# A hybrid SSD/attention layer with a convolutional FFN: TensorE's order ahead of the FFN written by hand

## The chip, the cores and the metric

One core of a Trainium2 chip runs the whole program in one launch. The metric is the device time of an execution in microseconds; of the kernel before there are three timed runs and one profiled execution.

## What is computed

One inference step of a one-layer streaming encoder for two groups of requests that share weights: a prompt of 2048 frames, and a sample group of 8 streams with 16 frames each and 512 cached positions. All data is float32.

```python
n = rmsnorm(x, norm1_g)
z, xbc, dt_raw, q, k, v, f_raw = split_columns(n @ w_in)     # 1024 -> 512,1024,8,512,512,512,8
y_ssd = ssd_mixer(z, xbc, dt_raw, ...)    # conv of width 4, SiLU, Mamba-2 scan (8 heads, state 128), gated norm
logf  = log_sigmoid(f_raw + fox_f_bias)
y_fox = softmax(q k' / 8 + F_q - F_k, causal) v              # F = cumsum(logf); 8 heads of 64
h = x + concat(y_ssd, y_fox) @ w_out
u = causal_dwconv(rmsnorm(h, norm2_g) @ w_up)                # 1024 -> 2 x 2816, width 3
y = rmsnorm(h + (silu(u_g) * u_v) @ w_down, final_norm_g)
# also returned: new k, v, logf, SSD state and both conv states of either group
```

## The kernel before

The 2048 prompt frames and the 128 sample frames (16 x 8) are 17 tiles of 128 rows; tile SMP holds the sample frames. Ahead of the FFN the prompt is worked in four parts of 512 rows (two windows of 256; the sample tile rides with part 0). Each matrix product with weights is done as three matmuls, high by high, high by low and low by high of operands split in two (`split`, one copy and one subtraction).

For each part p:
- `a_head(p)`: norm of the rows, written as high and low into the tiles nT0 and nT1 (one buffer each). A sum of squares per tile (ScalarE), a power on POOL, a scaled identity `dg`, a matmul that spreads it over partitions (line 196), a multiply with the transposed rows xT (line 202), the split.
- `a_body(p)`, first half: `proj_tm` (v and the gate columns, token-major, lines 344 to 346), `gates` (softplus, log-sigmoid and cumulative sums by a chain of small VectorE operations and small matmuls, lines 244 to 323), and `proj_cm` for four pairs of q and k (column-major, through `mm3`, lines 114 to 116). q and k go to DRAM as high and low.
- `attention(p)`: for each of 8 heads `s_phase` computes scores with queries on partitions (line 589) to get each row's maximum (line 592), which is transposed (603), copied out (605), stored to DRAM in st_d (606) and fetched back into row 66 and 67 of the q tile (607), so that `t_phase` gets transposed scores with the maximum already subtracted (629, 630), takes the exponential on ScalarE (636) and weighs v two units late (618). A unit is one block of 128 keys by 512 queries; a head of part p has 4(p+1). The PSUM tag s has four buffers, pv one, mm three. `ssd_chunk` steps (scan of one tile; for SMP a loop over 8 states in the tag yl) are issued between the units.
- for part 0, `sample_attention` behind the part's attention: per sequence, scores against 512 cached and 16 new keys, exponential, four transposes (757), weighing (768).
- `a_body(p)`, second half: `proj_cm` for 8 tiles of x with the convolution, `proj_tm` for z.

Then w_out is loaded and `out_proj` runs over the tiles, and the FFN follows in three groups of tiles (w_up, convolution, SiLU, w_down).

The order of every engine's queue, TensorE's too, is chosen when the kernel is built: a planner takes the traced instructions, with the order of tracing as priority, and simulates their times. Loads of data, stores and fetches all go through SP's DMA queue; weights go through ScalarE's.

Of the kernel before, what the change touches and what calls it, by code (L numbers as in the profile page):

```python
# [17 lines left out]
P = 128  # L18
# [9 lines left out]
H = 8  # L28
# [22 lines left out]
XB = 1  # L51
QB = 4
PB = 4
# [13 lines left out]
def hybrid_step(ctx: ExitStack, tc: tile.TileContext, i: dict, o: dict):  # L67
# [17 lines left out]
    st_d = dram.tile([H, 4, 2, 512], F32, name="st_d")  # L85
# [67 lines left out]
    def a_head(p, prev):  # L153
        res = []
        first = p == 0
        for e, w in enumerate(part_windows(p)):
            W = win_width(w, PAD1)
            wt = at([P, 2, KT, W], f"nT{e}", 1, F32R)
            if prev is None:
                V.memset(wt[:, :, :, 0:PAD1].bitcast(F32), 0.0)  # L160
            else:
                pw, pt = prev
                ed = PAD1 + pw[1] - pw[0]
                V.tensor_copy(wt[:, :, :, 0:PAD1], pt[:, :, :, ed - PAD1:ed].bitcast(F32))
            groups = [(w[0] // P, 2, PAD1, i["xTw"][w[0] // 256])]
            if w[2]:
                sb = PAD1 + w[1] - w[0]
                groups.append((SMP, 1, sb, i["xTs"]))
            for c0, n, col, xsrc in groups:
                N = n * P  # L170
                pr = tpt()
                if first:
                    xa = at([P, 2, KT, P], "cmw", WA).rearrange("p c k d -> p c (k d)")
                    for c in range(n):
                        nc.scalar.dma_start(xa[:, c], i["xr"][c0 + c])
                xTs = []
                for kk in range(0, KT, 4):
                    xT = at([P, 4, 256], "qk" if first else "xT", 2 if first else 1)
                    if first:
                        dma(xT[:, :, :N], xsrc[:, kk:kk + 4])  # L180
                    xTs.append(xT)
                for c in range(n):
                    ss = at([P, 2], "ss", 2)
                    if first:
                        S.activation(xa[:, c], xa[:, c], AF.Square, accum_out=ss[:, 0:1])
                    else:
                        for hf in range(2):
                            xt = at([P, 512], "xt", XB)
                            dA(xt, i["xr"][c0 + c][:, hf * 512:(hf + 1) * 512])
                            S.activation(xt, xt, AF.Square, accum_out=ss[:, hf:hf + 1])  # L190
                        V.tensor_add(ss[:, 0:1], ss[:, 0:1], ss[:, 1:2])
                    ss = ss[:, 0:1]
                    rsq(ss, D)
                    dg = at([P, P], "dg", 1)
                    V.tensor_scalar_mul(dg, ident, ss)
                    T.matmul(pr[:, c * P:(c + 1) * P], ones, dg, start=True, stop=True)
                for kk in range(0, KT, 4):
                    xT = xTs[kk // 4]
                    if not first:
                        dma(xT[:, :, :N], xsrc[:, kk:kk + 4])  # L200
                    for k in range(4):
                        V.scalar_tensor_tensor(xT[:, k, :N], xT[:, k, :N], g1c[:, kk + k:kk + k + 1], pr[:, :N],
                                               op0=ALU.mult, op1=ALU.mult)
                    split(xT[:, :, :N], wt[:, 0, kk:kk + 4, col:col + N], wt[:, 1, kk:kk + 4, col:col + N], S,
                          V if first and kk else G)
            prev = (w, wt)
            res.append(prev)
        wins_of[p] = res
        return prev

    def gates(p, dtf):
# [29 lines left out]
        if p == 0:  # L241
            dS(o["logf"][:, SMP], lf[:, 4])
        pc = tpt()
# [16 lines left out]

        an = at([P, 40], "g_an", 1)
# [14 lines left out]
        split(nf.rearrange("p c h -> p (c h)"), nh[:, 0], nh[:, 1], V, V)  # L276
        for a in range(2):
# [5 lines left out]
            dS(k2_d[:, 64 + a, p * 512:(p + 1) * 512], fr)  # L283
        if p > 0:
            return
# [6 lines left out]
        clf = at([P, 512], "xT", 1)  # L292
# [13 lines left out]
        split(snf.rearrange("p b h c -> p (b h c)"), snh[:, 0], snh[:, 1], V, V)  # L306
        pr = tpt()
        for a in range(4):
            T.transpose(pr[:, a * P:(a + 1) * P], snh[:, a // 2, (a % 2) * P:(a % 2 + 1) * P].bitcast(F32), ident)
        snr = at([P, 512], "xT", 1)  # L310
# [9 lines left out]
        split(ow, owh[:, 0], owh[:, 1], V, V)  # L320
        pr = tpt()
# [4 lines left out]
    def a_body(p):  # L326

        wins = wins_of[p]

        def proj_tm(src, n, use):  # L330
# [7 lines left out]
            for w, wt in wins:  # L338
                for c in win_tiles(w):
                    ps = mmt()  # L340
                    a = PAD1 + (c * P if c != SMP else w[1]) - w[0]
                    for k in range(KT):
# [3 lines left out]
                        T.matmul(ps[:, :n], wt[:, 1, k, a:a + P], we[:, 0, :n], start=False, stop=k == KT - 1)  # L346
                    use(ps, c)

# [31 lines left out]
        def proj_cm(ct, use, pad):  # L380
            wc = load_cm(ct)
            for w, wt in wins:
                W = win_width(w, PAD1) - PAD1 + pad
                ps = mmt()
                mm3(ps, lambda k: wc[:, 0, k, :], lambda k: wc[:, 1, k, :], wt[:, :, :, PAD1 - pad:], W, KT)
                use(ps, w, W)

# [56 lines left out]
        for pair in range(4):  # L444
            proj_cm(pair, use_qk(0, pair), 0)
            proj_cm(4 + pair, use_qk(1, pair), 0)
        yield
        for ct in range(8):
            proj_cm(8 + ct, use_x(ct), PAD1)
        proj_tm(i["w_tm"][1], 256, use_z(0))  # L450
        proj_tm(i["w_tm"][2], 256, use_z(1))
        if p == NPART - 1:
            dS(o["conv1"], cs1)
        yield


    def ssd_chunk(c):
# [51 lines left out]
        else:  # L509
            for b in range(NB):  # L510
                yield
# [5 lines left out]
                              xb[:, 6:8].rearrange("p g (t b) -> p g t b", b=NB)[:, :, :, b])  # L517
                for g in range(2):
                    T.matmul(po[:, g * 256:(g + 1) * 256], cm[:, g], s0[:, g * 256:(g + 1) * 256],
                             start=b == 0 and g == 0, stop=b == NB - 1 and g == 1, skip_group_check=True)  # L520
                xeb = bt_([P, 512], "pr", PB)
                V.tensor_scalar_mul(xeb, xe, blkb[:, b:b + 1])
# [56 lines left out]
    def s_phase(h, qb, done):  # L579

        q12 = load_q(h, qb)
        nm = bt_([P, 4, 4], "nm", 2)
        for kb in range(qb + 1):
            ks = load_ks(h, kb)
            for qi in range(4):
                W = (qi + 1) * P if kb == qb else 512
# [25 lines left out]
    def t_phase(h, qb, q12, yl, dn):  # L612
        pv = psb.tile([P, 512], F32, tag="pv", name="pv", bufs=1)
        order = [qb] + list(range(qb))
        late = []

        def weigh(vr, jj, of, pr, first, last):
# [571 lines left out]
```

## Time and profile before

| | us |
|---|---|
| median of 3 runs | 3202.15 (3199.07 to 3204.54) |
| the profiled execution, whole | 3197.92 |
| its span, first to last instruction | 3196.2 |
| TensorE busy | 3030.4 (95%) |
| VectorE busy | 1787.8 (56%) |
| ScalarE busy | 1029.7 (32%) |
| POOL busy | 899.0 (28%) |

Matmuls are pipelined and their ends modelled, so busy matmul time is not matmul time at peak. "Idle" is time with no matmul in flight. The granted clock of a stretch is a mean over two levels, 1.00 (2.4 GHz) and 0.50 (1.2 GHz). The span holds two halves: the stages ahead of the FFN up to about 1600 us, and the FFN.

### The profile page before, as it was taken

The page shows a single profiled execution, that of the slowest core. Times are in us where ns is not written, and L with a number is a line of the kernel's source. Part 1 is how long each engine was busy: PE and PEld are TensorE (multiplying, and loading weights), DVE is VectorE, ACT ScalarE, POOL GpSimd, SP SyncE. Part 2 cuts the span into 40 slices and gives each one's busy share as a digit, 9 for nine tenths or more (in the row PEclk, how much of TensorE's full clock was granted, in tenths as well). Part 3 has the DMA queues.
Part 4 walks back from the last instruction along what each step waited for, and adds up shares of the span by engine and source line. Part 5 has one row for each costly group of instructions (what it writes and reads, how often), then busy time and mean ns, then how long its engine had stood idle before and what let it go on. Part 6 is the DMA issues. An engine that isn't in the chain of part 4 may idle for free.

```text
span 3196.2 us, 45570 instructions
## 1 busy us (share of the span) xinstructions
PE 3030.4 (95%) x17712; PEld 2671.9 (84%) x17712; DVE 1787.8 (56%) x3315; ACT 1029.7 (32%) x1778; POOL 899.0 (28%) x580
## 2 busy tenths in 40 slices
PE   3999799798999998999999999999999999999999
PEld 3987688577777875777799999999999999999998
DVE  5175346654664465452455555566555556766666
ACT  2344333433444344322232222234222223422322
POOL 3222232322232323110132322223232222333332
PEclk8999899899999999999999999999999999999999
DMA  3757675646454746542621221223121221322221
GB/s 134 221 178 231 207 214 172 183 145 197 149 162 139 216 143 187 163 156 96 234 90 55 75 60 62 67 84 115 53 66 60 73 60 67 112 80 79 68 70 68
DMA packets 234495, 398.63 MB, mean 125 GB/s; under 512 B 62944, under 2 KB 119144, under 8 KB 234280
## 3 DMA queue, kind: packets, MB, share of 16 engines
q1 hardware_dynamic: 180712, 234.48, 23.3%
q10 hardware_dynamic: 53568, 161.24, 16.1%
q8 instruction: 140, 2.29, 0.3%
q14 instruction: 75, 0.61, 0.1%
HBM read 317.26 MB, written 78.38 MB: 124 GB/s over the span
## 4 chain that ended last, share of the span: by engine, by line
PE 83%; DMA 10%; DVE 4%; issue 1%; SPq 1%; ACT 1%; POOL 0%; ACTq 0%; DVEq 0%; POOLq 0%
PE mm L115 14%; PE mm L114 14%; PE mm L116 14%; PE pv L618 6%; PE dn L904 5%; PE dn L905 5%; PE dn L906 5%; PE s L629 2%; PE s L630 2%; PE dn L804 2%; PE dn L805 2%; PE dn L806 2%; PE mm L346 2%; PE s L589 2%; PE mm L344 2%; PE mm L345 2%
## 5 line engine op out<-in xcount | busy, mean ns | idle before, releaser
L106 POOL TENSOR_TENSOR wr<-raw,wr 128x1024 fp32r<-128x1024 f32 x198 | 476.4, 2414 | 1032.5 <-ACT wr L103 1025.0
L114 PE MATMUL mm<-nT,wr 128*128 128x386 f32 (+1 forms) x2112 | 696.4, 330 | 1.3 <-ACT wr L103 0.8
L115 PE MATMUL mm<-nT,wr 128*128 128x386 f32 (+1 forms) x2112 | 695.3, 329 | 0.1
L116 PE MATMUL mm<-nT,wr 128*128 128x386 f32 (+1 forms) x2112 | 694.4, 329 | 0.0
L882 DVE SCALAR_TENSOR_TENSOR ac<-mm,cw,ac 128x384 f32<-128x384 f32 (+1 forms) x528 | 301.6, 572 | 345.0 <-ACT ac L880 337.3
L880 ACT ACTIVATE ac<-mm,cw 128x384 f32<-128x384 f32 (+1 forms) x264 | 172.8, 654 | 786.1 <-PE mm L116 783.5
L115 PEld LDWEIGHTS mm<-nT,wr 128*128 128x128 f32 x2112 | 399.3, 189 | 6.8 <-DVE nT L106 0.3
L907 DVE TENSOR_TENSOR y<-y,dn 128x512 f32<-128x512 f32 x374 | 255.1, 684 | 267.3 <-PE dn L906 264.6
L114 PEld LDWEIGHTS mm<-nT,wr 128*128 128x128 f32 x2112 | 397.5, 188 | 7.7 <-ACT wr L103 1.1
L116 PEld LDWEIGHTS mm<-nT,wr 128*128 128x128 f32 x2112 | 397.9, 188 | 5.7
L106 POOL TENSOR_TENSOR cmw<-craw,cmw 128x1024 fp32r<-128x1024 f32 (+1 forms) x96 | 232.3, 2422 | 378.0 <-ACT cmw L103 304.8
L114 PE MATMUL mm<-nT,cmw 128*128 128x256 f32 (+2 forms) x1024 | 307.7, 300 | 1.8 <-ACT ev L400 1.8
L116 PE MATMUL mm<-nT,cmw 128*128 128x256 f32 (+2 forms) x1024 | 305.4, 298 | 0.0
L115 PE MATMUL mm<-nT,cmw 128*128 128x256 f32 (+2 forms) x1024 | 305.4, 298 | 0.0
L904 PE MATMUL dn<-wr,ht 128*128 128x512 f32 x748 | 294.4, 394 | 2.9 <-DVE y L907 1.7
L618 PE MATMUL pv<-pr,v 128*128 128x512 f32 (+3 forms) x640 | 291.9, 548 | 2.6 <-issue 1.4
L905 PE MATMUL dn<-wr,ht 128*128 128x512 f32 x748 | 292.8, 391 | 0.0
L906 PE MATMUL dn<-wr,ht 128*128 128x512 f32 x748 | 290.1, 391 | 0.0
L592 DVE TENSOR_REDUCE nm<-s 128x1 f32<-128x512 f32 (+2 forms) x320 | 190.9, 603 | 122.0 <-PE s L589 72.1
L103 ACT CAST wr<-raw 128x1024 fp32r<-128x1024 f32 x198 | 203.2, 1042 | 172.9 <-PE dn L906 161.4
L636 ACT ACTIVATE pr<-s 128x512 f32<-128x512 f32 (+1 forms) x320 | 166.1, 532 | 267.9 <-PE s L630 198.6
L114 PEld LDWEIGHTS mm<-nT,cmw 128*128 128x128 f32 x1024 | 196.6, 192 | 8.8 <-issue 4.8
(288 smaller groups left out, 5155.1 us busy)
## 6 DMA issues: line engine op xcount, KB each, us to landing
raw<-in_w_up ACTq DMA_DIRECT2D x132, 512.0 KB
raw<-in_w_down ACTq DMA_DIRECT2D x66, 512.0 KB
craw<-in_w_cm ACTq DMA_DIRECT2D x64, 512.0 KB
k<-k_d SPq DMA_DIRECT2D x80, 256.0 KB
craw<-in_w_tm ACTq DMA_DIRECT2D x24, 512.0 KB
q_d<-qk SPq DMA_DIRECT2D x96, 128.0 KB
k_d<-qk SPq DMA_DIRECT2D x96, 128.0 KB
ks<-k_d SPq DMA_DIRECT2D x80, 136.0 KB
```

The source lines that it names most:

```text
L103: S.copy(hi, src)
L106: leng.tensor_sub(lo, src, hi.bitcast(F32))
L114: T.matmul(ps[:, :W], whi(k), wt[:, 0, k, :W], start=k == 0, stop=False)
L115: T.matmul(ps[:, :W], whi(k), wt[:, 1, k, :W], start=False, stop=False)
L116: T.matmul(ps[:, :W], wlo(k), wt[:, 0, k, :W], start=False, stop=k == n - 1)
L592: V.tensor_reduce(nm[:, qi, kb:kb + 1], ps[:, :W], op=ALU.max, axis=AX.X, negate=True)
L618: m = T.matmul(pv[:, of:512], vr[:, jj], pr[:, :512 - of], start=first, stop=last)
L882: V.scalar_tensor_tensor(ac[:, 0:n], ps[:, j:j + n], cw2[:, ct, j:j + 1], ac[:, 0:n], op0=ALU.mult, op1=ALU.add)
L904: T.matmul(ps, ht[:, 0, ts_], wd[:, 0, cc], start=x == 0, stop=False)
L905: T.matmul(ps, ht[:, 0, ts_], wd[:, 1, cc], start=False, stop=False)
L906: T.matmul(ps, ht[:, 1, ts_], wd[:, 0, cc], start=False, stop=x == len(g) - 1)
L907: V.tensor_add(ys_[c][:, cc], ys_[c][:, cc], ps)
```

## The change

A block `manual_schedule` around everything from the first projection to the end of attention holds TensorE's queue to the order of tracing; the other engines are still planned. The order is made by a loop over the attention units of all four parts. Per unit it issues the unit, then the steps that are due of the side chain (sample attention in part 0, SSD chunks later), then pieces of projections while a credit, topped up per unit by `fill`, is above zero. "wait" stops the pieces for four units. The score phase runs one head and `LEAD` units ahead, over part boundaries.

To be issued in pieces, `proj_tm`, `proj_cm` and `out_proj` yield their cost in us after each half of the contraction (for `out_proj` after every second k), `gates` is cut into segments that are advanced before each q or k tile, `sample_attention` into five steps per sequence. `a_head` is split into `sizes` (for the next part, during the x pieces) and `rows`. The fetch of the row maxima through DRAM is replaced: maxima are written into columns 66 and 67 of a tile of 68 columns per query block, and four transposes bring them to partitions 66 and 67, from where a copy puts them into the q tile; this is issued two units into the next head's scores. Weighings left over from a head run in the next one's units. Buffers: xt 1 to 2, pr 4 to 5, dg 1 to 4; xT takes the tag qk.

```diff
+        for t in todo:
+            ds.append(sizes(*t))
+        yield 0.0
+        for t, d in zip(todo, ds):
+            rows(*t, d)
+            yield 0.0
...
-        proj_tm(i["w_tm0"], 272, use_v(1))
-        gates(p, dtf)
-        proj_tm(i["w_tm"][0], 256, use_v(0))
+        yield from proj_tm(i["w_tm0"], 272, use_v(1))
+        gs = gates(p, dtf)
+        next(gs)
+        yield from proj_tm(i["w_tm"][0], 256, use_v(0))
...
         for pair in range(4):
-            proj_cm(pair, use_qk(0, pair), 0)
-            proj_cm(4 + pair, use_qk(1, pair), 0)
-        yield
+            for ct, kind in ((pair, 0), (4 + pair, 1)):
+                next(gs, None)
+                yield from proj_cm(ct, use_qk(kind, pair), 0)
+        yield None
...
-        mh = bt_([P, 2, 4], "mh", 2, F32R)
-        split(M, mh[:, 0], mh[:, 1], V, V)
-        pt = pss()
-        T.transpose(pt[0:8, 0:128], mh.rearrange("p a c -> p (a c)").bitcast(F32), ident)
-        rr = bt_([8, P], "rr", 2)
-        V.tensor_copy(rr, pt[0:8, 0:128])
-        dS(st_d[h, qb].rearrange("a (c p) -> (a c) p", p=P), rr)
-        dma(q12[66:68, 1].bitcast(F32), st_d[h, qb])
-        done.append(q12)
+        mh = mhs[h % 2]
+        split(M, mh[:, :, 66], mh[:, :, 67], V, V)
+
+        def shift():
+            pt = pss()
+            for c in range(4):
+                T.transpose(pt[0:68, c * P:(c + 1) * P], mh[:, c].bitcast(F32), ident)
+            V.tensor_copy(q12[64:68, 1], pt[64:68])
+            done.append(q12)
+
+        rest.append(shift)
...
+            for _ in t_phase(h, p, done[n], yl, dn):
+                k += 1
+                while at_s < cum + size[n] + nxt * k // size[n] + LEAD:
+                    next(ahead, None)
+                    at_s += 1
+                yield p
...
+    def part_steps(p):
+
+        body = bodies[p]
+        hd = a_head(p + 1) if p + 1 < NPART else None
+        for k, c in enumerate(body):
+            if c is None:
+                break
+            if k == 12 and hd:
+                next(hd)
+            yield c
+        if not hd:
+            return
+        next(hd)
+        yield "wait"
+        next(hd)
+        for c in hd:
+            pass
+        bodies.append(a_body(p + 1))
+        for c in bodies[p + 1]:
+            if c is None:
+                return
+            yield c
+
+    def out_steps():
+        A.close()
+        open_out()
+        psum["wo"] = out_weights()
+        yield "wait"
+        yield "wait"
+        yield "wait"
+        for c in [SMP] + list(range(11)):
+            yield from out_proj(c)
...
+    fill = [(0, 157.0, 20), (1, 140.0, 80), (2, 140.0, 172), (3, 69.0, 216), (4, 132.0, 318)]
+    sides = {0: (sample_attention, 5 * NB + 1), 1: (lambda: chunks(SMP, 0, 1, 2, 3), 66), 2: (lambda: chunks(4, 5, 6, 7), 40),
+             3: (lambda: chunks(*range(8, 16)), 80)}
+
+    with tc.manual_schedule(engines={nc.tensor.engine}):
...
+        for u in att:
+            if u is None:
+                credit += 1.5
+            else:
...
+                n += 1
+                cnt += 1
+                while given < total * cnt // (32 * (u + 1)):
+                    next(side, None)
+                    given += 1
+                if hold:
+                    hold -= 1
+                    continue
+                if gen is not None:
+                    start = fill[stage - 1][2] if stage else 0
+                    credit += fill[stage][1] / (fill[stage][2] - start)
+            while gen is not None and credit > 0 and not hold:
+                c = next(gen, None)
+                if c is None:
+                    stage += 1
+                    gen = (part_steps(stage) if stage < NPART else out_steps()) if stage < len(fill) else None
+                elif c == "wait":
+                    hold = 4
+                else:
+                    credit -= c
```

## Rows read from the trace of the kernel before

**Rows 1.** The page: span, TensorE's busy time, granted clock in 40 slices.
```profile
span 3196.2 us, 45570 instructions
...
PE 3030.4 (95%) x17712; PEld 2671.9 (84%) x17712; DVE 1787.8 (56%) x3315; ACT 1029.7 (32%) x1778; POOL 899.0 (28%) x580
...
PEclk8999899899999999999999999999999999999999
```

**Rows 2.** By stretch: length, busy of PE, PEld, DVE, ACT, POOL, clock, DMA, GB/s.
```profile
57.50:79.70 22.20, 7.55 (x30) 5.11 (x29) 15.51 (x57) 2.74 (x10) 4.60 (x2) 0.57 0.17 57
80.00:1600.00 1520.00, 1418.77 (x8916) 1161.62 (x8915) 778.37 (x1603) 543.81 (x1077) 382.11 (x299) 0.96 0.57 179
...
296.00:372.00 76.00, 54.69 (x510) 39.04 (x509) 39.78 (x143) 24.29 (x59) 21.93 (x16) 0.78 0.71 240
...
557.00:670.00 113.00, 91.28 (x507) 65.62 (x505) 82.14 (x171) 45.06 (x99) 40.12 (x38) 0.88 0.56 167
...
760.00:830.00 70.00, 56.74 (x344) 46.37 (x343) 37.20 (x73) 24.40 (x48) 15.82 (x10) 0.88 0.46 135
...
1230.00:1285.00 55.00, 42.35 (x166) 25.06 (x164) 25.05 (x39) 23.69 (x38) 24.56 (x17) 0.88 0.67 207
1285.00:1500.00 215.00, 215.00 (x1018) 158.33 (x1017) 95.60 (x149) 60.54 (x115) 19.23 (x33) 1.00 0.46 148
1500.00:1600.00 100.00, 93.81 (x422) 76.74 (x421) 38.96 (x58) 25.87 (x50) 12.83 (x15) 0.97 0.55 197
1600.00:3196.20 1596.20, 1583.58 (x8641) 1486.09 (x8639) 964.03 (x1587) 465.50 (x666) 490.99 (x248) 1.00 0.23 73
```

**Rows 3.** The same view, one stretch at the lower clock.
```profile
60.40:84.30 23.90, 11.87 (x49) 9.64 (x50) 14.21 (x57) 2.15 (x10) 1.70 (x1) 0.50 0.22 71
```

**Rows 4.** TensorE's waits: who waited for whom, total us, times, longest us.
```profile
PE tp L196 <- DVE dg L195: 39.8, 8, 16.1
PE s L630 <- DMA q<-st_d: 15.9, 3, 8.5
PE s L757 <- ACT pr L751: 10.5, 4, 3.2
PE tp L244 <- DVE g_ld L237: 10.2, 2, 9.6
PE s L589 <- DVE rr L605: 8.8, 2, 6.4
PE mm L344 <- ACT nT L103: 7.5, 4, 4.3
...
PE mm L344 <- DVE xT L202: 6.6, 3, 3.8
```

**Rows 5.** Groups by line (busy, mean ns), then two runs in the chain (start, us).
```profile
L603 PE MATMUL s<-ident,mh 128*8 128x128 f32 x32 | 8.9, 278 | 4.4 <-DVE mh L106 4.3
L282 DVE COPY g_2k<-tp 8x512 f32<-8x512 f32 x8 | 5.4, 678 | 9.9 <-DMA k_d<-g_2k 4.3 <-PE mm L345 3.2 <-PE tp L280 2.3
...
1378.02 1.72 PE pv L618 x4
...
1569.68 1.75 PE tp L858 x16
```

**Rows 6.** SP's waits (as rows 4), and one store in the chain.
```profile
SPq L607 <- DMA st_d<-rr: 62.2, 28, 5.0
...
443.28 9.43 DMA st_d<-rr
```

**Rows 7.** The chain: weighings of two following sample sequences.
```profile
283.53 1.36 PE s L768 x40
...
298.05 1.36 PE s L768 x40
```

**Rows 8.** The chain: store of one sample state, load of the next into its buffer.
```profile
484.04 4.65 DMA out_s_ssdT<-yl
488.70 2.54 DMA yl<-in_s0T
```

More of the change, by code (lines that the diff above doesn't have):

```diff
@@ L165, in a_head @@
             groups = [(w[0] // P, 2, PAD1, i["xTw"][w[0] // 256])]
             if w[2]:
[L167 to L171, printed above, removed]
-                if first:
[L173 to L205, printed above, removed]
@@ L211, in gates @@
+        ds = []
+        if first:
+            for t in todo:
+                rows(*t, sizes(*t))
+            yield 0.0
+            return
+        for t in todo:
+            ds.append(sizes(*t))
+        yield 0.0
+        for t, d in zip(todo, ds):
+            rows(*t, d)
+            yield 0.0
     def gates(p, dtf):
@@ L577, in load_q, with s_phase @@
         return q12
-    def s_phase(h, qb, done):
+    mhs = [cb.tile([P, 4, 68], F32R, name=f"mh{e}") for e in range(2)]
+    for mh in mhs:
+        V.memset(mh[:, :, 0:64].bitcast(F32), 0.0)
+        V.memset(mh[:, :, 64:66].bitcast(F32), 1.0)
+    def s_phase(h, qb, done, rest):
         q12 = load_q(h, qb)
         nm = bt_([P, 4, 4], "nm", 2)
+        n = 0
         for kb in range(qb + 1):
@@ L585, in s_phase @@
             for qi in range(4):
+                if n == 2 and rest:
+                    rest.pop()()
+                n += 1
                 W = (qi + 1) * P if kb == qb else 512
@@ L643, in t_phase @@
-        S.copy(yl[rs], pv[rs])
-        S.copy(dn[rs], pv[ot])
-        if e:
-            for a in range(4):
-                cc = slice(a * P, (a + 1) * P)
-                V.reciprocal(dn[:, cc], dn[:, cc])
-            V.tensor_mul(yl, yl, dn)
-            dS(mix_d[4 * qb:4 * qb + 4, :, 4 + h // 2, :].rearrange("c p t -> p c t"), yl.rearrange("p (c t) -> p c t", t=P))
-    def attention(p, others):
-        done = []
+                first = kb == qb and jj == 0
+                while len(late) >= (3 if late and late[0][0] == "first" else 2):
+                    kind, a, x = late.pop(0)
+                    if kind == "first":
+                        a.append(psb.tile([P, 512], F32, tag="pv", name="pv", bufs=1))
+                    weigh(a[0], *x)
@@ L657, in scores, with t_rest, attention @@
+                late.append(("first" if first else "", pv, (vr, jj, of, pr, first, kb == order[-1] and jj == 3, end)))
+                yield
+    def t_rest():
+        while late:
+            kind, a, x = late.pop(0)
+            weigh(a[0], *x)
+    def attention():
+        done, rest = [], []
+        heads = [(p, h) for p in range(NPART) for h in range(H)]
+        size = [4 * (p + 1) for p, h in heads]
         def scores():
-            for h in range(H):
-                yield from s_phase(h, p, done)
+            for p, h in heads:
+                yield from s_phase(h, p, done, rest)
+            rest.pop()()
@@ L661, in attention @@
         ahead = scores()
-        for h in range(H):
-            while len(done) <= h:
-                next(ahead, None)
-            if h == 0:
-                for _ in range(LEAD):
-                    next(ahead, None)
-            if h % 4 == 0:
-                side = (None for g, _ in others[h // 4] for _ in g)
-                total = sum(n for _, n in others[h // 4])
-                units = 4 * 4 * (p + 1)
-                k, given = 0, 0
+        at_s, cum = 0, 0
+        for n, (p, h) in enumerate(heads):
```

228 lines of the change are left out of this document (154 added, 74 removed).

## The prediction

> **What bounds the kernel now.** I read the page first. TensorE is busy for 95% of a span of 3196.2 us [rows 1], so either its work or its standing still sets the time. In the clock line the reader should see that its losses lie in the first half, ahead of the FFN. The views by stretch come next. From 1600 us on it is busy for 1583.6 of 1596.2 us at a granted clock of 1.00 [rows 2]: the FFN, which the change leaves alone, has nothing to give. From 80 to 1600 us it is idle for 1520 - 1418.8 = 101.2 us, at a mean clock of 0.96 [rows 2]. The clock has two levels, so 0.96 means that about 2 x 0.04 x 1520 = 122 us ran at the lower one, 1.2 GHz. It falls behind the longer stops, and work goes on at half pace: for 11.9 us of the 23.9 us around the gates' stop [rows 3]. If two thirds of the 122 us hold work (half did there), the clock costs 122 x 2/3 x 1/2 = 40 us (30 to 50). From 57.5 to 79.7 us the gates of part 0 leave it idle for 14.7 us, and the slow clock takes another 11.9 / 2 = 6. The loss within reach is 101 + 40 + 21 = 162 us. The start-up before that, 39.8 us of waits for the first rows' scaled identity dg [rows 4], stays.
>
> By stretch, idle time plus a third of the low-clock time, from [rows 2]: 57.5 to 79.7 (gates of part 0) 21; 296 to 372 (sample attention, head of part 1) 21.3 + 11 = 32; 557 to 670 (head of part 2) 21.7 + 9 = 31; 760 to 830 (score phases) 13.3 + 5.6 = 19; 1230 to 1285 (loading w_out) 12.7 + 4.4 = 17; 1500 to 1600 (end of attention) 6.2 + 2 = 8. That is 128; the other 34 are spread out. The list of waits names causes: row maxima fetched back from DRAM and their evacuation rr (15.9 + 8.8 us), the next part's rows nT and xT (7.5 + 6.6), the sample rows' exponentials (10.5) [rows 4]. That TensorE can run such mixed stages without loss is shown by 1285 to 1500 us: busy for 215 of 215 us at clock 1.00, with attention, SSD and output projection by turns [rows 2].
>
> **The change part by part.** (a) *Order.* TensorE's queue is traced and no longer planned: after each attention unit (scores for the maxima, transposed scores, a weighing some units late) come the side chain's due steps and as many projection pieces as the credits allow. The matmuls are those of before, so the order adds no work. Credits: 157 us over 20 units, 140 over 60, 140 over 92, 69 over 44, 132 over 102, so nearly every unit has 1.3 to 7.9 us of projections beside it.
>
> (b) *Gates.* Each part's vector chain is cut into segments behind a 256-column projection or one q or k tile. The 21 us of part 0 were exactly such a chain without cover; its longest wait was 9.6 us [rows 4], and the diff prices a q or k tile of part 0 at (256 + 384) x 0.011 = 7.0 us. I keep 4 us and gain 17 (bounds 10 to 20).
>
> (c) *Heads.* The next part's sizes are computed among the x pieces, its rows before and after four units that get no pieces; xt gets a second buffer, half of the split goes from POOL to VectorE. The nT tiles stay single, so the rows can't start until part p's last z matmul is done. Waits on rows were up to 4.3 us each [rows 4]; four units cover one window, and the second window's loads wait for the first one's buffers. Of the 31 us I keep 8. The xr loads go on SP's queue earlier and may wait there for an xt buffer; k, v and q loads stand behind them, briefly, by the second buffer.
>
> (d) *Row maxima.* The store to st_d and the fetch back are gone: 64 DMAs of SP, which stood before the fetch for 62.2 us in 28 waits with later k and v loads behind it; one store took 9.4 us on the chain [rows 6]. In place of one transpose of 8 columns there are four of 68 per head and part, 3 x 32 = 96 more. Sixteen transposes in a row took 1.75 us [rows 5], so 96 x 0.109 = +10.5 us on TensorE; by the 278 ns of one alone [rows 5] it is 27 us. I take the lower, as four follow one another. The copy out is 4 rows of 512 columns: by the 678 ns of an 8x512 copy [rows 5] at most 32 x 0.68 = 22 us of VectorE, which is busy for 778 of 1520 us [rows 2] and hides it; late, it would hold up the next head's transposed scores. The transposes are issued two score units into the next head, so the split of the maxima has two units to finish. Of the 19 us I keep 4.
>
> (e) *Sample attention* runs in 41 steps among the 32 units of part 0 instead of behind them. Before, one sequence followed another after 298.05 - 283.53 = 14.5 us [rows 7]; now each has four units with projections between its steps. Of the 32 us I keep 10. *w_out* is loaded behind twelve units without pieces: of 17 I keep 3. The *end* keeps its 8. Of the spread 34 I keep 15, as round trips and gates of later parts are in it.
>
> (f) *New waits.* A late operand now stops everything behind it on TensorE: the next unit, its exponential on ScalarE, its maximum on VectorE, and through the buffers SP's loads. One place is plain: the sample chunk's state update has one step a unit, and a state's buffer turns over in a store of 4.65 and a load of 2.54 us [rows 8], with matmuls and two vector operations between, some 11 us in all. A unit of part 1 is about 0.86 (a weighing, half of 1.72 [rows 5]) + 0.7 (three score matmuls at the diff's 1.36 / 6) + 140 / 60 = 2.3 of pieces + the step, 5 to 5.5 us. With two free buffers of the tag yl that fits; while a head pair holds one, each step waits some 5 us. For a third of the eight steps, 10 us (0 to 45). For all other new waits I take 6 (0 to 60).
>
> *Sum.* Kept: 4 + 8 + 4 + 10 + 3 + 8 + 15 = 52, so 110 of 162 go; new are 10.5 + 10 + 6 = 26.5. Net 83.5. The profiled execution took 3197.9 us around its span of 3196.2, 4.2 under the runs' median of 3202.15, so its successor is 3114 and a median 3118; I say 3116.
>
> One rule of the skill speaks against the change. TensorE stood 8.5 us for one late row of maxima [rows 4], and nothing from further back in its queue was run meanwhile. The Trainium skill, "TensorE: Matmul & The Clock Gate", section "Part 2: What happens when you issue a matmul", says that only weight loads are pulled ahead while matmuls stay in program order. The trace agrees by that row; by the rule a hand order is as good as its slowest operand, and the sum would come out as in rival 3.
>
> **The rivals.**
> 1. *Nearly all of it goes.* For: the 215 us without loss [rows 2]. Then the gates' 4, the end's 8, the transposes' 10.5 and some 15 remain: 3202 - 162 + 37.5 = 3077. Against: in that stretch no rows waited for a single buffer and no state was being swapped.
> 2. *The idle time comes back elsewhere.* SP's, VectorE's and ScalarE's orders are still planned from estimated times, and the waits in rows 4 end on those and on DMAs, which are busy for 0.57 to 0.71 of the time in these stages [rows 2]; pressed together, loads land later. Then only the gates (17), the round trips (15, and 8 in the spread part) and some of the heads (12) go: 52 - 26.5 = 25.5, so 3176. Against: the largest stalls are chains that had nothing traced beside them.
> 3. *The other side: sample attention stops TensorE in every sequence.* A sequence takes four k12 buffers, attention holds one of the four, so a sequence's last load waits for matmuls of its own first step, and the next one's for its weighing; in a fixed order TensorE can't go round. If it stands for the whole 14.5 us of [rows 7] less some 3 us of the sequence's own matmuls, 8 x 11.5 = 92 us plus 12 of clock come on top of 3116: 3220. It decides from 86 / 8 = 10.8 us per sequence on. Against: four units with up to 7.9 us of pieces each are longer than 14.5 us.
> 4. *It doesn't do what it says:* the planner's order was in effect this one already, and the time stays within 0.2%. Against: the idle stretches in rows 2.
>
> **How the numbers follow.** Forecast 0.52 (its own range 3090 to 3150), rival 1 0.20, rival 2 0.16, rival 3 0.09, rival 4 0.03. The range runs from 22 below rival 1 (the clock's 50, the 15 gone too) to 12 above rival 2 (the transposes' upper bound): 3055 to 3188. It leaves out rivals 3 and 4 and a little of each end. A change below 0.2%, 6.4 us, can't be told from none here. Faster: 0.52 + 0.20 + 0.15 = 0.87; same 0.03; slower 0.10, rival 3 and 0.01 of rival 2.
>
> **What would show it.** Right: the FFN begins some 80 us earlier and lasts as long; TensorE's idle time between start-up and there is 35 to 60 us, its clock 0.98 or more; no wait on a fetched maximum; the gates' gap gone. Wrong: waits of over 3 us on states, k12 loads or nT that come back once per sequence or unit; four transposes that cost clearly over 0.5 us a head; or an FFN of another length.

## The result and the profile after

Over four runs the changed kernel took 3181.23 us (median; 3180.02 to 3183.61), the kernel before 3202.88 (3199.07 to 3204.54). The ratio is 0.9935, its 95% interval 0.9918 to 0.9952. The forecast was 3116: the sign was right, and a quarter of the gain came, 21.6 us of 87.

The page of the changed kernel, for [rows 1]: span, TensorE's row, its granted clock in 40 slices.

```profile
span 3178.3 us, 45508 instructions
...
PE 3035.1 (95%) x17808; PEld 2671.8 (84%) x17808; DVE 1829.3 (58%) x3325; ACT 1024.1 (32%) x1778; POOL 882.4 (28%) x574
...
PEclk9998988999999998999999999999999999999999
```

The view by stretch of the changed kernel, with the columns of [rows 2].

```profile
57.50:79.70 22.20, 21.66 (x171) 21.38 (x170) 13.77 (x40) 6.00 (x18) 7.91 (x4) 1.00 0.51 153
80.00:1576.10 1496.10, 1402.39 (x8830) 1138.26 (x8829) 819.22 (x1624) 531.66 (x1066) 355.54 (x289) 0.96 0.58 179
240.00:320.00 80.00, 68.58 (x527) 55.34 (x527) 42.28 (x115) 28.81 (x64) 24.27 (x18) 0.85 0.59 192
400.00:560.00 160.00, 132.74 (x880) 109.20 (x881) 89.18 (x190) 44.77 (x93) 28.84 (x20) 0.87 0.53 163
720.00:800.00 80.00, 80.00 (x526) 65.03 (x525) 57.35 (x108) 34.45 (x66) 19.66 (x14) 1.00 0.59 169
...
1200.00:1280.00 80.00, 67.50 (x273) 46.24 (x274) 40.74 (x52) 27.17 (x46) 22.44 (x18) 0.83 0.52 162
...
1576.10:3178.30 1602.20, 1588.77 (x8669) 1491.04 (x8667) 964.98 (x1589) 467.54 (x668) 496.13 (x250) 1.00 0.24 73
```

The same stretches of the kernel before, cut where its FFN begins:

```profile
80.00:1594.00 1514.00, 1413.55 (x8888) 1156.73 (x8887) 777.42 (x1602) 541.33 (x1074) 376.43 (x297) 0.96 0.57 179
1594.00:3196.20 1602.20, 1588.81 (x8669) 1490.98 (x8667) 964.98 (x1589) 467.98 (x668) 496.68 (x250) 1.00 0.23 73
```

The last 1602.2 us of either trace hold the same 8669 matmuls, so the FFN starts at 1576.1 us instead of 1594.0 and lasts as long as before. The whole gain of these two executions is the 17.9 us ahead of it. The first row is the gates' stop of part 0: TensorE, idle for 14.7 us of these 22.2 before [rows 2], now works through 21.66 of them at clock 1.00. With the slow clock that went too, this one place is about as large as the whole gain. From 80 us on little is better: 93.7 us idle against 100.4, at a mean clock of 0.96 in both. The losses stand elsewhere now: 240 to 320 (11.4 us idle, clock 0.85), 400 to 560 (27.3 idle, 0.87), 1200 to 1280 (12.5 idle, 0.83). Between them lie stretches without any.

TensorE's waits in the changed kernel, for [rows 4].

```profile
PE tp L203 <- DVE dg L184: 35.5, 5, 14.8
PE s L555 <- DMA yl<-in_s0T: 13.8, 4, 4.3
PE s L530 <- DVE xd L521: 7.2, 2, 6.2
PE s L832 <- DVE bs L826: 7.1, 1, 7.1
PE s L634 <- DMA q<-q_d: 7.0, 2, 4.3
PE s L530 <- issue: 6.3, 1, 6.3
```

The first row is the start-up. Of those that led [rows 4], the fetched maximum and nT ahead of the projections have gone, and the exponential of the sample rows (now L820) is down to 1.9 us. L555, the wait for the next sample state, was 2.7 us in the kernel before and is 13.8. L530 (an SSD step) and the copy bs at L832 (a sample sequence) stood in no row of before.

**A short copy that stops TensorE.** TensorE in the changed kernel at 260 us (start, length, work, idle time before it):

```profile
259.67 0.60 PE L651 MATMUL s<-ident,mh 128*68 128x128 f32 x4
260.02 0.42 PE L634 MATMUL s<-ks,q 68*128 68x384 f32 x1
...
261.64 1.08 PE L832 MATMUL s<-k,pr 128*32 128x128 f32 x32 [0.35 <-ACT pr L822]
269.82 0.65 PE L832 MATMUL s<-yl,bs 16*32 16x128 f32 x8 [7.10 <-DVE bs L826]
```

VectorE in the same stretch of the same kernel:

```profile
258.37 3.39 DVE L680 RECIPROCAL rdb<-rdb 128x128 f32<-128x128 f32 x4 [0.57 <-ACT rdb L676]
...
263.61 2.03 DVE L208 SCALAR_TENSOR_TENSOR qk<-qk,g1c,tp 128x256 f32<-128x256 f32 x5
265.57 2.10 DVE L184 TENSOR_SCALAR dg<-ident,ss 128x128 f32<-128x128 f32 x1
...
269.49 0.27 DVE L826 COPY bs<-s 16x128 f32<-16x128 f32 x1
```

The last eight small matmuls of a sample sequence need a copy of 0.27 us of what the transpose ahead of them (L824) left at 261.3 us. In VectorE's planned queue it stands behind the head of part 1 and four shorter operations, 7.8 us of work from 261.67 on, so TensorE stands for 7.10 us. The eight matmuls are not the whole of it: one of the four is L652, which copies the maxima out for the q tile, and in e6 below, where the next attention unit goes ahead of those eight, it is this unit that stands, for L652 (L657 there):

```profile
264.75 0.47 PE L698 MATMUL s<-q,k 128*128 128x128 f32 x1 [5.73 <-DVE q L657]
```

In e1, where the planner puts matmuls of a projection there as well, 2.2 us for L652 are left. In the changed kernel the stop costs again behind it, in the clock of the next 20 us:

```profile
269.80:290.00 20.20, 16.95 (x92) 9.80 (x96) 7.41 (x27) 5.75 (x15) 2.72 (x5) 0.58 0.68 231
```

**A queue that holds another.** SP (DMA issues), then ScalarE, in the changed kernel from 447 us on, where an SSD step of part 1 stands in TensorE's order:

```profile
449.14 6.97 SPq L844 DMA_DIRECT2D mix_d<-sg  x7
...
460.45 0.34 SPq L498 DMA_DIRECT2D sg<-ac_d  x1
```

```profile
460.15 0.28 ACT L697 ACTIVATE pr<-s 128x128 f32<-128x128 f32 x1
469.54 1.06 ACT L501 ACTIVATE sg<-sg 128x1024 f32<-128x1024 f32 x1 [9.11 <-DVE sg L500]
...
472.44 0.58 ACT L697 ACTIVATE pr<-s 128x512 f32<-128x512 f32 x1
```

The decay sg of an SSD chunk is loaded behind seven stores of the sample rows, into the buffer that they read. ScalarE then waits 9.11 us for it (the load, then a step each on POOL and VectorE), with the exponentials of attention behind it in its queue; TensorE's 6.3 us at L530, the step that multiplies by this decay, end at 473.4.

### The profile page after: what moved, and what is told of

Its sections match the earlier page's. It is cut to its first block, busy times and chain, and to the rows that moved or that the text cites. A ratio compares the mean times of both kernels' runs of the same rounds, so it can differ in the third digit from the quotient of the medians.

```text
span 3178.3 us, 45508 instructions
## 1 busy us (share of the span) xinstructions
PE 3035.1 (95%) x17808; PEld 2671.8 (84%) x17808; DVE 1829.3 (58%) x3325; ACT 1024.1 (32%) x1778; POOL 882.4 (28%) x574
## 3 DMA queue, kind: packets, MB, share of 16 engines
q1 hardware_dynamic: 180072, 234.22, 23.9%
## 4 chain that ended last, share of the span: by engine, by line
PE 84%; DMA 7%; DVE 4%; issue 2%; SPq 1%; POOL 1%; ACT 1%; ACTq 0%; POOLq 0%; DVEq 0%
PE mm L113 11%; PE mm L114 11%; PE mm L115 11%; PE pv L662 6%; PE dn L975 5%; PE dn L976 5%; PE dn L977 5%; PE mm L413 3%; PE mm L414 3%; PE mm L415 3%; PE dn L873 2%; PE mm L366 2%; PE dn L875 2%; PE mm L367 2%; PE dn L874 2%; PE mm L368 2%
## 5 line engine op out<-in xcount | busy, mean ns | idle before, releaser
L413 PE MATMUL mm<-nT,cmw 128*128 128x256 f32 (+2 forms) x1024 | 309.2, 302 | 1.6 <-DVE g_2k L300 1.6
L414 PE MATMUL mm<-nT,cmw 128*128 128x256 f32 (+2 forms) x1024 | 298.6, 292 | 0.0
L415 PE MATMUL mm<-nT,cmw 128*128 128x256 f32 (+2 forms) x1024 | 297.9, 291 | 0.0
L634 PE MATMUL s<-ks,q 68*128 68x512 f32 (+2 forms) x320 | 201.4, 635 | 10.8 <-DMA q<-q_d 7.0
```

Of the source, the lines that this page charges most:

```text
L413: T.matmul(ps[:, :W], wc[:, 0, k, :], wk[:, 0], start=k == 0, stop=False)
L414: T.matmul(ps[:, :W], wc[:, 0, k, :], wk[:, 1], start=False, stop=False)
L415: T.matmul(ps[:, :W], wc[:, 1, k, :], wk[:, 0], start=False, stop=k == KT - 1)
```

## The experiments

Ratios are to the kernel before in the same batch; differences in us are between medians. The median of the kernel before moves by up to 4.5 us from batch to batch (3202.88 to 3207.37), so such a difference is good to some 5 us.

**e1: the order planned again.** All else of the change stays.

```diff
-    with tc.manual_schedule(engines={nc.tensor.engine}):
+    with ExitStack():
```

> The changed kernel with the block that fixes TensorE's order taken away: the same program in the same order of tracing, but TensorE's queue is planned again like the others. Theory H (the new waits come from the fixed order: a late step of a side chain stops everything behind it): the planner puts other matmuls in place of the late steps, the gates, the transposes and the early heads stay, so it is faster than the changed kernel, 3140 to 3170 us. Theory Q (the waits come from the queues of SP and ScalarE, where a late transfer holds up all that is behind it, however TensorE's queue is made): within 10 us of the changed kernel's 3181, or slower.

Measured 3135.22 us (3126.3 to 3136.95), ratio 0.9769 [0.9751, 0.9787]: 46 us faster than with the hand-written order, a little beyond what H gave. By stretch e1 shows:

```profile
80.00:1522.40 1442.40, 1379.18 (x8832) 1128.74 (x8831) 820.73 (x1625) 532.25 (x1067) 356.74 (x289) 0.98 0.61 186
...
1522.40:3124.60 1602.20, 1588.79 (x8669) 1491.04 (x8667) 965.58 (x1589) 467.64 (x668) 496.54 (x250) 1.00 0.24 73
```

Idle time between 80 us and the FFN is 63.2 us instead of 93.7, and the clock is higher (the trace is of e1's fastest execution, 3126.3). So the hand-written order costs 46 us against the planned one (53 by the ratios), and the other parts of the change gain 68. The planner makes the other engines' orders anew for each kernel: the 46 us belong to TensorE's order together with the plans that it leads to.

**e2, e3: two buffers.** e2 gives the tag yl a third buffer (room for it from another pool); e3 takes the sample rows' result ys out of the buffer that sg uses.

```diff
-                s0 = bt_([P, 512], "yl", 2)
+                s0 = bt_([P, 512], "yl", 3)        # e2, at each place of the tag
-        ys = bt_([64, 8, P], "sg", 1)
+        ys = at([64, 8, P], "ys", 1)               # e3 alone
```

> The changed kernel with three buffers instead of two for the tag that the sample states share with the attention output (one small constant moves to another pool to make room). Theory H: the four waits of 2.3 to 4.3 us for a state's load between 500 and 544 us and the low clock behind them go, about 14 + 8 us: 3160 us. Theory Q: the loads stand in SP's queue behind other waits, so at most a third of that goes: 3174 to 3181 us.

> The changed kernel with the sample attention's output in a tile of its own, so that the first SSD chunk's decay tile can be loaded without waiting for that output's eight stores. Theory H: the decay chain of the sample chunk starts some 10 us earlier and the stop of 6.3 us at 473 us goes with its low clock: 3170 us. Theory Q: the load still stands behind the same eight stores in SP's queue, which took 7 us there: 3178 to 3183 us.

e2: 3159.88 us (3153.64 to 3167.88), ratio 0.9857 [0.9832, 0.9882]; L555's waits are gone from the list. The state buffer costs the hand-written order 21 us. Its trace up to the FFN, to be set against 1496.10 us with 1402.39 of work:

```profile
80.00:1552.20 1472.20, 1392.66 (x8836) 1132.18 (x8835) 817.95 (x1625) 533.24 (x1067) 354.99 (x289) 0.97 0.60 182
```

Of the 23.9 us between the two, 14.2 are idle time and 9.7 are the same matmuls at a higher clock.

e3: 3182.88 us, ratio 0.9926 [0.9911, 0.9941], no gain. The time is the one that Q gave, but not by Q's mechanism: the load of the first chunk's decay is now issued at 151.22 us, ahead of all the stores, and the 6.3 us at L530 that ended at 473.4 are gone. The stop comes back one chunk later, where the next decay is loaded into the same buffer and ScalarE waits for it in the same way (ScalarE, then TensorE, in e3):

```profile
485.77 1.06 ACT L501 ACTIVATE sg<-sg 128x1024 f32<-128x1024 f32 x1 [6.84 <-DVE sg L500]
```

```profile
487.37 2.07 PE L559 MATMUL s<-pr,bs 128*128 128x256 f32 x4 [6.67 <-ACT pr L697]
```

So taking away this one stop gained nothing; what stays is the decay's place in ScalarE's planned queue.

**e4: the kernel before, with transposed maxima alone** (st_d removed, four transposes of 68 columns, its own planned order).

> The kernel before with one part of the change alone: the row maxima are moved by four transposes and a copy instead of the store to and fetch from DRAM; TensorE's order is planned as before. Both theories have 10.5 us of added transposes. By the forecast's terms the round trips were worth 15 us of the 19 and 8 of the spread part: 3202 - 23 + 10.5 = 3190 us. Theory Q gives more to it, since SP no longer stands 62 us in 28 waits with loads behind it: 3165 to 3185 us. If the round trips were hidden anyway: 3205 to 3213 us.

3197.58 us, ratio 0.996 [0.9942, 0.9977]: 8 us of gain, less than the 12 or more that either theory gave, and more than if the round trips had been hidden. In place of the fetch TensorE waits 21.4 us in eight times for the split of the maxima.

**e6: side chains planned, the rest by hand.** Sample attention and SSD steps are issued outside the fixed order; attention, projections, heads, gates and output projection keep it (each stretch of it is chained to the one before by its last matmul).

```diff
-                    next(side, None)
+                    free(lambda: next(side, None))   # leaves the fixed order and enters it again
```

> The changed kernel with TensorE's order still fixed for attention units, projection pieces, heads, gates and output projection, in the same order as before this edit, while the steps of the sample attention and the SSD chunks are left to the planner, which may put them at another place between those. Theory H1 (the 46 us that the fixed order costs against the planned one are waits for late steps of these side chains): most of it comes back, 3130 to 3150 us. Theory H2 (attention and projections themselves stand in the fixed order, for q loads, heads and w_out): 3165 to 3183 us.

3158.51 us (3155.4 to 3160.38), ratio 0.9856 [0.9832, 0.988]. 23 of the 46 us come back, between the two. TensorE's waits of e6 still have the states:

```profile
PE s L560 <- DMA yl<-in_s0T: 9.2, 4, 4.4
```

**e14: e6 with the third state buffer.**

> e6 (sample attention and SSD steps planned, all else in the fixed order) with the third state buffer of e2. Theory A (the 23 us that came back in e6 are the 21 us of e2 seen from the other side: what the side chains cost in a fixed order is the wait for states): 3152 to 3160 us, no less than e6 or e2 by more than 8. Theory B (they are different losses): 3135 to 3145.

3136.23 us (3135.41 to 3139.35), ratio 0.9784 [0.9766, 0.9801]: 45 us less than the changed kernel, 21 + 23, the time of e1. So e2 and e6 found different losses, and attention, pieces, heads and gates can keep the hand-written order at little cost (9 us against e7 below, with intervals that still overlap). The stretches of e14 that were the worst of the changed kernel:

```profile
240.00:320.00 80.00, 73.04 (x582) 60.53 (x581) 48.10 (x131) 31.61 (x70) 26.65 (x20) 0.89 0.66 210
400.00:560.00 160.00, 140.66 (x1013) 118.97 (x1011) 115.45 (x230) 57.99 (x118) 43.07 (x33) 0.95 0.61 188
```

**e7: e1 with the third state buffer.**

> The planned order of e1 with three buffers for the tag of the sample states. With the fixed order the third buffer was worth 21 us. Theory H1 (a late state costs much only where nothing else may go first): worth 5 us or less here, 3130 to 3137 us. If a late state costs the same in any order: 3112 to 3118 us.

3127.25 us (3125.56 to 3129.62), ratio 0.9762 [0.9742, 0.9782], the fastest kernel here and below both. The buffer that is worth 21 us in the fixed order gives 8 at most in a planned one, whose interval overlaps e1's.

**e9: SSD steps further apart** (three empty steps more in each chunk).

> The changed kernel, order fixed, with three empty steps more in each SSD chunk: two between its loads and its first transposes, one ahead of the eight-head matmuls, so that its matmuls come later in the fixed order than their operands were asked for (the steps of a part are spread over the same units). Theory H1 with distance as the cure: the stops of 6.3 and 6.2 us ahead of the eight-head matmuls and those ahead of later transposes shrink, with their low clock: 3155 to 3170 us. If the operands are late because of the queue they stand in and not for want of distance: 3175 to 3190 us.

3189.4 us, ratio 0.9954 [0.9939, 0.9968]: no gain (8 us more than the changed kernel by the medians, with intervals that overlap). The stops that it was aimed at went all the same: ahead of the eight-head matmuls (L533 here) 1.4 us are left of 7.2 + 6.3. Others grew, for the states (13.8 before, L558 here) and ahead of the chunk's last step (6.1 before, L582 here):

```profile
PE s L558 <- DMA yl<-in_s0T: 19.7, 5, 7.0
PE s L582 <- DVE yt L578: 15.4, 5, 6.1
...
PE s L533 <- DVE sg L517: 1.4, 1, 1.4
```

The steps of part 1 are spread over the same 64 units, 81 of them in place of 66, so the empty ones push the others together. Distance for one operand was taken from the others; that this is the whole reason is not shown.

**e12, e15: where in time.** e12 plans parts 0 and 1 and fixes the order from part 2 on; e15 is the reverse.

```diff
-    with tc.manual_schedule(engines={nc.tensor.engine}):
+    with ExitStack() as pin:
...
                 if u != side_p:
+                    if u == 2:
+                        pin.enter_context(tc.manual_schedule(engines={nc.tensor.engine}))
```

> TensorE's order planned through parts 0 and 1 of the attention and fixed as in after from the first weighing of part 2 on. The fixed order cost 46 us in all. Theory A (the cost lies where side chains and heads follow each other closely, in the first 640 us: there e1 is ahead by 38 us of TensorE's work, and behind by some 8 between 640 and 1200): 3140 to 3150 us. Theory B (a fixed order costs by the number of its steps: two thirds of the attention's units stand behind that place): 3160 to 3172.

> The complement of e12: TensorE's order fixed as in after through parts 0 and 1, planned from the first weighing of part 2 on. Theory A (the fixed order costs where it stands, stage by stage, and 36 of the 46 us lie in parts 0 and 1): 3166 to 3176 us, 5 to 15 less than after. Theory B (the two halves act on each other: a planned second half takes up what the first lost, or the reverse): below 3160, or no less than after.

e12: 3145.33 us, ratio 0.9806 [0.9783, 0.9828]. e15: 3174.25, ratio 0.9901 [0.9885, 0.9917]. By e12 parts 0 and 1 hold 36 of the 46 us, by e15 the rest holds 7; together 43. Most of the loss lies where it stands, in the first 600 us or so, in which sample attention, the sample states and two heads follow each other.

**e13: other engines by hand too.** In one kernel VectorE and ScalarE, in another SP, are put in the order of the program beside TensorE.

```diff
-    with tc.manual_schedule(engines={nc.tensor.engine}):
+    with tc.manual_schedule(engines={nc.tensor.engine, nc.sync.engine}):
```

> As after, and VectorE's and ScalarE's orders ahead of the FFN are written by hand too (each in the order in which the program names its instructions), SP's and GpSimd's stay planned. Theory A (the loss of the fixed order comes from orders that do not belong together: TensorE's by hand, VectorE's and ScalarE's planned, so that short copies stand behind instructions of a later step): the wait at L832 for the 0.27 us copy goes, and 10 to 30 of the 46 us come back, 3151 to 3171 us. Theory B (it is TensorE's own order that is wrong: a step stands in it at a place its data has not reached): no gain, 3176 to 3186, or slower, 3187 to 3230, where an instruction that waits now holds up others on these engines too.

> As after, and SP's order (loads and stores ahead of the FFN) by hand too, in the order of the program. Theory A (SP's planned order puts stores ahead of loads that a step of the fixed order needs): L555's waits on its state loads (13.8 us) and the wait behind the eight mix_d stores shrink, 3155 to 3172 us. Theory B (the order of SP is not at fault; the loads are late because their buffers come free late, and in program order a load that waits for its buffer holds up those behind it): 3178 to 3186, or slower.

4131.92 us (ratio 1.2894 [1.2863, 1.2924]) and 4120.08 us (1.2853 [1.2826, 1.288]): the sign of B, and both theories far off in size. TensorE's order is the changed kernel's but for some of the output projections. What it waits for, with VectorE and ScalarE by hand:

```profile
PE mm L413 <- ACT cmw L102: 401.1, 63, 16.1
PE mm L366 <- ACT cmw L102: 118.7, 15, 11.2
```

and with SP by hand, together with a piece of SP's queue at 300 us:

```profile
PE s L692 <- DMA k<-k_d: 383.4, 58, 19.0
PE s L634 <- DMA ks<-k_d: 137.6, 46, 13.3
```

```profile
300.14 18.41 SPq L391 DMA_DIRECT2D z_d<-ev  x6
318.65 0.38 SPq L589 DMA_DIRECT2D k<-k_d  x1
```

In the order of the program a weight tile's cast and a load of k no longer run ahead of what comes before them. Six stores that wait for their data hold SP for 18.41 us, with the load of k behind. So the planned orders of these engines carry the lead of loads and casts, some 940 us of it. Whether another order of these engines, neither planned apart nor that of the program, would give the 46 us back is not tested.

**e8, e10, e11: single terms of the sum, in the planned order of e1.** e8 runs the gates in one piece; e10 fetches the maxima back from DRAM; e11 runs each head in one piece.

```diff
         gs = gates(p, dtf)
-        next(gs)
+        for _ in gs:                     # e8
+            pass
...
-        for t in todo:                   # e11: sizes and rows of a window together
-            ds.append(sizes(*t))
...
+        for t in todo:
+            rows(*t, sizes(*t))
```

> The planned order of e1 with each part's gates traced in one piece behind the first projection, as in the kernel before. In part 0 the planner has no attention to put there, so by the forecast's term of 17 us and the 20 us that the trace of the changed kernel showed at this place: 3150 to 3160 us. If the gates are covered by projections anyway, once they may be planned among the pieces: 3133 to 3140 us.

> TensorE's order planned as in e1, and the row maxima of the score phases go to DRAM and back as in the kernel before (one transpose per phase instead of four). Theory A (the prediction's term: nine waits and their slow clock, 19 to 25 us, go, and the transposes cost 10.4): 3144 to 3152 us, 9 to 17 more than e1 (3135), with waits of TensorE on the fetched queries. Theory B (ahead of the FFN the planner has other work to put there, so that the fetch stops nothing): the time falls by the transposes, 3125 to 3130. In between, 3131 to 3143: what they save pays for them and not much more.

> TensorE's order planned as in e1, but each part's head in one piece again: sums of squares, scales and rows of the normalised input follow each other, none issued ahead. Theory A (the prediction's term: the heads' waits, 23 us of 31, went by issuing the sizes ahead): 3153 to 3162 us. Theory B (the planner pulls the sizes forward by itself, so that the split in pieces matters to a fixed order alone): 3130 to 3140, as e1.

e8: 3169.88 us (3166.21 to 3170.6), ratio 0.9892 [0.9872, 0.9912], 35 us more than e1. The wait at the gates' first transposes is back in it, with the 9.6 us that it had in [rows 4]:

```profile
PE tp L260 <- DVE g_ld L252: 9.6, 1, 9.6
```

Its first 80 us, and then the same of e1:

```profile
0.00:80.00 80.00, 29.36 (x164) 25.72 (x165) 46.49 (x131) 20.36 (x36) 25.89 (x34) 0.90 0.40 136
```

```profile
0.00:80.00 80.00, 43.34 (x311) 42.09 (x312) 44.84 (x113) 24.66 (x45) 30.74 (x36) 1.00 0.49 160
```

The gates of part 0 are 14.0 us of idle time there, and the clock is lower. TensorE waits for over 0.3 us ahead of no matmul of the gates of parts 1 to 3, so where the rest of the 35 us comes from is not shown: e8's whole plan differs from e1's. e10: 3142.82 us (3134.9 to 3147.6), ratio 0.98 [0.9777, 0.9822], 8 us more than e1, the middle case, with intervals that overlap; TensorE waits 6.9 us in three times on st_d. e11: 3141.29 us (3136.82 to 3142.8), ratio 0.9795 [0.9777, 0.9813], 6 us more, again with intervals that overlap, a little above theory B and far from A: the planner makes up for most of the split by itself.

**e16: w_out off ScalarE,** on top of e7.

```diff
-            dW(raw, i["w_out"][0, k * P:(k + 1) * P, :])
+            dma(raw, i["w_out"][0, k * P:(k + 1) * P, :])
...
-            split(raw, w[:, 0], w[:, 1], S, G)
+            split(raw, w[:, 0], w[:, 1], G, G)
```

> e7 (planned order, three state buffers) with ScalarE freed of w_out: its eight pieces are loaded by SP and not by ScalarE's queue, and their cast runs on GpSimd and not on ScalarE. In e7 TensorE is idle for 12.2 us of the 80 from 1120 to 1200, as before the change, and ScalarE waits 11.6 us there for pieces of w_out with exponentials behind. Theory A (the head of ScalarE's queue stops the attention): 3112 to 3121 us, with most of the 12.2 us gone. Theory B (the stage is short of other work for TensorE, or GpSimd's 35 us of casts and subtractions hold up the SSD's steps as much): 3123 to 3132, as e7 (3127).

3140.64 us (3135.47 to 3141.69), ratio 0.9791 [0.9777, 0.9806]: 13 us slower than e7 by the medians, with intervals that just touch; both theories missed. Its longest waits of TensorE after the start-up are in that stage:

```profile
PE s L579 <- DVE yt L575: 12.2, 3, 9.8
PE dn L873 <- ACT mx L102: 8.9, 1, 8.9
```

An SSD step and the first output projection now stand for 9.8 and 8.9 us at a time. Ahead of the first, VectorE waits for one of the SSD's small powers on GpSimd, which ran there at 1166.25, behind casts and a subtraction of w_out:

```profile
1166.98 2.94 DVE L575 SCALAR_TENSOR_TENSOR yt<-yt,ss,ngB 128x256 f32<-128x256 f32 x2 [8.01 <-POOL ss L109]
```

GpSimd is no better place for these casts than ScalarE. The loads moved to SP's queue in the same edit, and what share they have is not told apart. What would cure the stage stays open.

## Why the prediction was wrong

The step that failed is (f), *new waits*: priced at 16 us, measured at 46. Beside it two of the "kept" shares, in (c) and (e), failed. Of the signs of being wrong that were on record, waits of over 3 us on states came (L555, up to 4.3 us), and TensorE's idle time is 93.7 us, not 35 to 60. The forecast, by term, with what was measured (single terms in the planned order, where they need not add up exactly):

| term | forecast | measured | by |
|---|---|---|---|
| gates | +17 | +35 | e8 |
| heads | +23 | +6 | e11 |
| row maxima less transposes | +15 - 10.5 | +8 | e10, e4 |
| w_out stage | +14 | about 0 | by stretch |
| sample attention and spread | +22 + 19 | 68 - 35 - 6 - 8 = 19 | remainder |
| new waits of the fixed order | -16 | -46 | e1 |
| sum | 83.5 | 22 | |

**(f) New waits.** The mechanism was named, the size was wrong: the state's buffer at 10 us costs 21 (e2), "all other new waits" at 6 cost some 25 (e6 and e14). I took the value near the lower end of 0 to 60, though nothing in the rows spoke for that end. Four of the eight states came late, by 13.8 us in all; I had a third of the eight late by some 5 each (13 by these factors, though I took 10), so the idle time was near, and what I left out is what follows such stops: work at the slower clock, 9.7 of e2's 23.9 us. A unit was also read too long: half of the 1.72 us in [rows 5] is two weighings, and a unit has one, 0.43. The rule of the Trainium skill that the prediction weighed (matmuls stay in program order; "TensorE: Matmul & The Clock Gate", "Part 2: What happens when you issue a matmul") agrees with the 7.10 us at L832. But the planned order of e1 is also a fixed sequence when it runs. What the hand order lacks, by e1, is steps that stand where the other queues bring their data.

**(b) Gates.** The 17 us were right for part 0: the first row by stretch and the 14.0 us of e8. The other 18 of e8's 35 us are not explained: I had put the gates of parts 1 to 3 among the 34 us spread out and counted half of these, but TensorE doesn't wait for them in e8.

**(c) Heads.** e11 gives 6 us, not 23. The wait on rows that [rows 4] shows goes mostly without the split: nT's 7.5 us are 1.1 in e1 and 1.0 in e11. The stall was real, but the split was not what removed it. The second xt buffer, the four of dg, xT's other tag and the half of the split on VectorE are all still in e11; which of them did it, or the new plan, is not told apart.

**(d) Row maxima.** Right: the fetch is gone from the waits, though 9.4 us of waits on maxima that come late are left (L651, L692 and L693), where I kept 4. Four transposes hold TensorE for 260.02 - 259.67 = 0.35 us, 32 times 11 us, near the 10.5 forecast and far from the 27.

**(e) w_out.** Of 17 us none went: 12.5 us idle from 1200 to 1280 in the changed kernel and 12.5 from 1120 to 1200 in e1, against 12.7 before [rows 2]. Units without pieces don't cover it. One reason is that the eight loads pass through two buffers and ScalarE's queue. In e1:

```profile
1155.05 1.04 ACT L102 CAST wo<-raw 128x1024 fp32r<-128x1024 f32 x1 [5.22 <-DMA raw<-in_w_out]
1156.00 0.59 ACT L697 ACTIVATE pr<-s 128x512 f32<-128x512 f32 x1
```

The cast waits 5.22 us for its load, an exponential stands behind it, and TensorE stands 3.11 us for that exponential. Waits on exponentials are 5.3 of the 12.5 us in e1. Most of the others there are for an SSD step and for the output projection's operands, and the longest in the changed kernel, 4.1 us, is for an SSD step.

**The rivals.** Rival 2's time, 3176, came within 5 us, but by luck: its sum gave the gates 17 and the heads 12, and the order no loss beyond the 16 us of (f). What it says of the idle time, that it comes back elsewhere, is what the stretches show, and its mechanism, queues that are planned apart, shows at L826 and L501. e13 shows that putting these queues in program order is no way out. Rival 3 fell: one sequence stops TensorE for 7.1 us, not eight for 11.5. Of the 68 us that the rest of the change gains, 19 are a remainder of four differences, each good to some 5 us, and are not told apart into sample attention and spread losses; that stays open. So does what the 23 us of the side chains without the states consist of, beyond the two places shown.

## What to carry to other kernels

Price a hand-written order per step: for each operand of a step, find the queue that delivers it, and what stands there ahead of it; a side chain that is issued into the plan while the main work keeps its order gave the whole loss back together with one more buffer. Before fixing an engine's order, run the same change with the order planned: here the generators, gates in pieces and transposes were worth 68 us, and the fixed order took 46 of them away. Don't credit a rearrangement with a stall that the planner may remove once anything else around it is moved. And a stop that goes away need not shorten the kernel: in e3 and e9 the stops aimed at went, and others took their place.

## What the runs showed of the hardware

TensorE stood 7.1 us for a 0.27 us copy, with 7.8 us of other work ahead of it in VectorE's queue. Stops of a few us cost again in the clock: behind that one the granted clock was 0.58 on the mean of 20 us, and e2, with 14.2 us less idle time, ran the same matmuls in 9.7 us less. And with TensorE's order nearly the same, SP's order alone, or VectorE's and ScalarE's together, moved the time by some 940 us, twenty times the 46 us that TensorE's own order moved.
